# Linear attention's v and r products with 512 moving columns, r multiplied in behind the transposes, and the last turns' transposes at other steps

## The chip, the cores and the metric

The kernel is one program on one core of a Trainium2 chip. The metric is device time in microseconds (us), the median of the runs shown. The engines are called TensorE (PE; its weight loads are PEld), VectorE (DVE), ScalarE (ACT), GpSimd (POOL) and SyncE (SP, which issues nearly all DMAs here).

## The reference, cut to what matters

One layer of a decoder trunk over 1024 tokens of width 1024. A normalised input h is projected once; two mixers, gated DeltaNet (GDN) and gated linear attention (GLA), use its columns; both are projected, merged by gates, projected again and added; an MLP with a squared relu follows. What the change touches most is GLA, with 4 heads, key width 128 and value width 256:

```python
def gla_branch(q, k, v, r, gate_lr, gate_w2, gate_b, norm_w):
    ...
    gate_logit = (gate_lr @ gate_w2.astype(gate_lr.dtype)).astype(jnp.float32) + gate_b.astype(jnp.float32)
    log_a = jax.nn.log_sigmoid(gate_logit) / GLA_TAU
    log_a = split_heads(log_a, GLA_HEADS, GLA_DK)
    o = gla_chunked(qh, kh, vh, log_a).transpose(0, 2, 1, 3)
    rg = jax.nn.silu(r.reshape(bsz, s, GLA_HEADS, GLA_DV).astype(jnp.float32))
    o = rms_norm_f32(o, norm_w) * rg
    return o.reshape(bsz, s, GLA_V).astype(q.dtype)
```

q, k, v, r and gate_lr (16 columns) are column blocks of h @ w_in. gla_chunked works through chunks of 64 tokens with a state of 128x256 per head. The MLP is `u = square(relu(h @ w_mlp_up))`, `x + rms_norm(u @ w_mlp_down)`, with h the normalised result of the mixer.

## The kernel before

Every large float32 product is made as three products of a high and a low part in the type F32R: high with high, high with low, low with high (`mm3`, L256). The parts of a weight slab are made on the chip: SP loads 256 KB into a buffer of `wraw` (4 of them), ScalarE casts it to `wh` (L237, in `split`), VectorE subtracts to get `wl` (L166 through `tt`). Of wh and wl there are three buffers each (`wsp`). The activations' parts are `hT` and `hL`, with features on the partitions and tokens along the row.

Two forms of product exist. In `gemm_fm_` the weights are stationary and 512 tokens move: the result has features on the partitions, and each slab feeds 24 matmuls of 128x512. In `gemm_tm_` (L305) a block of 128 tokens is stationary and 256 weight columns move: the result has tokens on the partitions, and each slab feeds 48 matmuls of 128x256. Results go to four PSUM banks called g; the rest of the work has one bank each called mt, ml, mr and mo.

The GLA part (from L783) runs two streams at once. The main stream is the projections in the order of GORDER (k0 is head 0's q and k, v0 and r0 its v and r, g5 a block of merge-gate logits). The other is the attention proper, woven in between by `drive` (L76) with a virtual clock of TensorE (`TensorClock`): `ball_pair` for two heads' decays (a product of the low-rank gate input `sm` with `gw2`, in float32 on L68; then an exponential and a logarithm over 128x2048 on ScalarE, `e1s`, and a running sum on VectorE), `gla_mix` for one head, `gla_out` for its output. A table `need` says which of these must be over before a projection is started.

For each head and each half u of the tokens, gla_mix makes the attention matrix, and in two groups g of two token blocks the output in bank mo or ml. Each group is then squared and summed on ScalarE (into `jk`, a discard), its inverse root is taken on GpSimd (`so`, L172 and L186), and VectorE multiplies the group by it and by silu(r) into `gr` (L175, tokens on the partitions). When a head is done, gla_out transposes gr (TensorE, L72), ScalarE scales it by the norm's weight (`ot`), and SP writes it to DRAM (`d_ob`).

After the mixer comes the turn stage. The normalised mixer output `m` (tokens on the partitions) is transposed for the MLP. `turn(u, i)` does that for one of eight token blocks: two groups of four transposes to banks mt and ml, then copies and differences on ScalarE and VectorE into blocks `R` (`hilo`, L1096), `X` and two of `big`. The up-projection is arranged by Strassen's scheme over halves, which is what the differences are for. The turns of the second half stand between the steps of a loop of 16 (P1 and P2, 12 matmuls of 128x512 a step, banks mr and mo), and TURNS names the steps: TURNS[0] for u=0 in the projection before, TURNS[1] for u=1 in the loop. After the loop `prep(0)` loads the first up-weights into a buffer `wu` that X had until then (L1073), sums them on VectorE (`ss`), and the next products start from their casts.

Of the kernel before, what the change touches and what calls it, by code (L numbers as in the profile page):

```python
# [16 lines left out]
P = 128  # L17
S = 1024
# [8 lines left out]
TURNS = (2, 5, 6, 9), (3, 6, 10, 12)  # L27
# [4 lines left out]
GORDER = "k0 v0 r0 k1 v1 r1 k2 v2 r2 k3 v3 r3 g5"  # L32
# [101 lines left out]
def kernel(  # L134
# [30 lines left out]
    def tt(out, a, b, op, eng=None):  # L165
        (eng or V).tensor_tensor(out=out, in0=a, in1=b, op=op)  # L166
# [162 lines left out]
    sm = gp.tile([112, S], F32, name="sm")  # L329
# [51 lines left out]
    def decays(cv):  # L381


        ws = cv.tile([P, KT, 24], F32, name="ws", tag="Xc")
# [393 lines left out]


    with tc.tile_pool(name="gl", bufs=1, reuse_waits="tile") as gl:  # L780

        reserve(gl, (("gq", 512, 3), ("gk", 512, 3), ("gvh", S, 3), ("gvl", S, 3), ("gr", S, 4)))
        gw2 = gl.tile([112, 512], F32, name="gw2")  # L783
        V.memset(gw2, 0.0)
        for r in (32, 96):
            SP.dma_start(out=gw2[r:r + 16, :], in_=gla_gate_w2[0])
# [10 lines left out]
        def ball_pair(hh):  # L797

            lap = ball.rearrange("p h (u i) -> p (h u) i", u=2)
            for n in range(4):  # L800
# [4 lines left out]
                T.matmul(pl_, gw2[:, h * P:(h + 1) * P], sm[:, u * 512:u * 512 + 512], start=True, stop=True)  # L805
# [22 lines left out]
        def gla_v(h):  # L828
            bvv = yield from gemm_tm_(win_slab(C_BV + h * 256), KT, hT, hL)
            vs = [[gl.tile([P, 4, 256], F32R, tag="gv" + x, name="gv" + x, bufs=3) for x in "hl"] for _ in range(2)]  # L830
            for j in range(4):
                hi, lo = (v_[:, (j % 2) * 2:(j % 2) * 2 + 2, :].rearrange("p t c -> p (t c)") for v_ in vs[j // 2])
                with tc.high_priority(offset=HPE):
                    A.copy(out=hi, in_=bvv[j])
                    tt(lo, bvv[j], hi.bitcast(F32), ALU.subtract)
            vg[h] = vs

        def gla_r(h):
            brr = yield from gemm_tm_(win_slab(C_BR + h * 256), KT, hT, hL)
            rr = [gl.tile([P, 4, 256], F32, tag="gr", name="gr", bufs=4) for _ in range(2)]  # L840
            for j in range(4):
                rt3 = rr[j // 2][:, (j % 2) * 2:(j % 2) * 2 + 2, :]
                rt = rt3.rearrange("p t c -> p (t c)")
                with tc.high_priority(offset=HPE):
                    act(rt, brr[j], AF.Tanh, scale=0.5)
                    stt(rt, rt, 1.0, brr[j], ALU.add, ALU.mult)
            rg[h] = rr

        def gla_mix(h, mark):
            (qs, ks), vs = qkg[h], vg[h]  # L850
            st = None
            for u in range(2):
# [55 lines left out]
                vH, vL = vs[u]  # L908
                so = gl.tile([P, 4], F32, tag="so", name="so", bufs=2)
                jk = gl.tile([P, 2, 256], F32, tag="ot", name="jk", bufs=1)  # L910
                for g in range(2):
# [11 lines left out]
                    for j in range(2):  # L923
# [5 lines left out]
                        if j < nd:  # L929
# [608 lines left out]
```

## Time and profile before

| what | value |
|---|---|
| runs | 1704.4 us median of 3 (1701.24 to 1704.83) |
| the profiled execution | 1699.28 us, span 1697.5 us |
| granted TensorE clock, mean | 0.994 |
| PE / DVE / ACT / POOL busy | 97% / 58% / 45% / 8% of the span |

A matmul's own duration is longer than the distance between the starts of two in a row, since they are pipelined. In the list of waits the columns are: engine and line, what it waited for, total us, times, longest us. In the timeline they are start, duration, engine, line, operation, output and inputs with shapes, and in brackets the idle time before and what ended it. In the groups they are minimum, median and maximum in ns, and first and last start in us. In the table by stretches they are the length, the busy time of each engine, the granted TensorE clock (PEclk, 1.00 at full speed), the DMA engines' busy share and GB/s. The GLA part lies at about 434 to 822 us, the turn stage's loop at 1060 to 1112 us.

### The profile page before, as it was taken

Reading aid. Unit: us, or ns where it says so; the run is one execution under the profiler, and the core shown is the slowest. Engines: PE = TensorE matmul, PEld = TensorE weight load, DVE = VectorE, ACT = ScalarE, POOL = GpSimd, SP = SyncE. Lnnn points to the kernel's source line nnn. Section 1 sums busy time; section 2 is a strip of 40 time slices with the busy share of each in tenths; the row PEclk is TensorE's granted clock in tenths of the full one; section 3 lists DMA queues with packets and bytes.
Section 4 is the critical chain, followed back from the end, with each engine's and each line's share of the span. In section 5 each row is a group of like instructions: output and inputs, shape, how many; then the busy total and the mean of one; then the engine's idle time right before and its main releaser. Section 6 shows DMA issues by size and latency. Waiting matters only on the chain.

```text
span 1697.5 us, 24475 instructions
## 1 busy us (share of the span) xinstructions
PE 1653.0 (97%) x9174; PEld 1403.0 (83%) x9174; DVE 987.2 (58%) x1678; ACT 771.5 (45%) x1576; POOL 135.9 (8%) x222
## 2 busy tenths in 40 slices
PE   7999999999999999999999999989999999999997
PEld 6888778878898989998888888778888878888886
DVE  5677565872445335643354545798777655564764
ACT  5456554643533335433421235654555555443442
POOL 3010111111001000001100011200000000000021
PEclk9999999999999999999999999999999999999999
DMA  5222213322211212122743345687678698786763
GB/s 168 56 73 76 84 38 90 92 59 67 79 45 38 69 43 58 38 63 87 235 150 97 111 159 174 212 263 231 205 258 281 240 334 307 243 272 221 249 224 136
DMA packets 186405, 251.39 MB, mean 148 GB/s; under 512 B 23351, under 2 KB 108430, under 8 KB 186286
## 3 DMA queue, kind: packets, MB, share of 16 engines
q1 hardware_dynamic: 186286, 249.83, 45.7%
q8 instruction: 72, 1.18, 0.3%
q14 instruction: 47, 0.39, 0.1%
HBM read 185.79 MB, written 63.98 MB: 147 GB/s over the span
## 4 chain that ended last, share of the span: by engine, by line
PE 82%; DVE 7%; DMA 4%; ACT 4%; issue 2%; POOL 1%; SPq 0%; DVEq 0%; ACTq 0%; POOLq 0%
PE g L68 58%; PE mr L68 8%; PE mo L68 7%; PE ml L68 4%; PE mt L68 3%; DMA gb<-d_g 2%; DVE Xt L166 1%; PE mt L72 1%; DVE Xi L548 1%; DVE wl L166 1%; ACT E L178 1%; DMA oraw<-d_oa 1%; ACT wh L237 0%; DMA rv<-in_w_mlp_down_dram 0%; ACT Zp L604 0%
## 5 line engine op out<-in xcount | busy, mean ns | idle before, releaser
L166 DVE TENSOR_TENSOR wl<-w,wh 128x512 fp32r<-128x512 f32 x181 | 125.6, 695 | 223.5 <-ACT wh L237 220.0
L68 PE MATMUL g<-hT,wh 128*128 128x512 f32 (+1 forms) x600 | 239.1, 399 | 1.2 <-DVE gr L175 0.9
L68 PE MATMUL g<-hL,wh 128*128 128x512 f32 (+1 forms) x600 | 232.8, 388 | 0.0
L68 PE MATMUL g<-hT,wl 128*128 128x512 f32 (+1 forms) x600 | 232.1, 387 | 0.0
L237 ACT CAST wh<-w 128x512 fp32r<-128x512 f32 x184 | 113.8, 619 | 208.0 <-PE g L68 175.0
L68 PE MATMUL g<-wh,hT 128*128 128x256 f32 x640 | 185.7, 290 | 0.0
L68 PE MATMUL g<-wl,hT 128*128 128x256 f32 x640 | 182.1, 284 | 0.0
L68 PE MATMUL g<-wh,hL 128*128 128x256 f32 x640 | 182.0, 284 | 0.0
L68 PE MATMUL g<-big 128*128 128x512 f32 x768 | 175.3, 389 | 1.7 <-ACT big L1231 1.6
L68 PEld LDWEIGHTS g<-big 128*128 128x128 f32 x768 | 144.0, 188 | 32.3 <-ACT big L1231 2.0
L166 DVE TENSOR_TENSOR big<-ru,big 128x1024 fp32r<-128x1024 f32 x53 | 64.9, 1225 | 114.6 <-ACT big L1231 114.2
L68 PEld LDWEIGHTS g<-hT,wl 128*128 128x128 f32 x600 | 113.4, 189 | 21.6 <-DVE wl L166 0.2
L68 PEld LDWEIGHTS g<-hT,wh 128*128 128x128 f32 x600 | 113.4, 189 | 21.5 <-DVE gr L175 1.1
L68 PEld LDWEIGHTS g<-hL,wh 128*128 128x128 f32 x600 | 113.8, 190 | 18.8 <-issue 1.0
L1231 ACT CAST big<-ru 128x1024 fp32r<-128x1024 f32 x53 | 55.8, 1053 | 153.1 <-PE g L68 56.6
L68 PEld LDWEIGHTS g<-wh,hT 128*128 128x128 f32 x640 | 123.1, 192 | 1.4 <-issue 1.0
L68 PEld LDWEIGHTS g<-wl,hT 128*128 128x128 f32 x640 | 123.2, 193 | 1.2 <-issue 1.0
L68 PEld LDWEIGHTS g<-wh,hL 128*128 128x128 f32 x640 | 123.1, 192 | 0.1
L68 PE MATMUL g<-wh,big 128*128 128x512 f32 x256 | 81.1, 393 | 0.2 <-DVE m L166 0.2
L68 PE MATMUL g<-big,wh 128*128 128x512 f32 x256 | 78.8, 389 | 0.0
L178 ACT ACTIVATE c<-c 128x512 f32<-128x512 f32 x104 | 64.1, 630 | 21.8 <-DVE c L166 20.1
L166 DVE TENSOR_TENSOR big<-rv,big 128x1024 fp32r<-128x1024 f32 x53 | 64.6, 1218 | 0.2
(450 smaller groups left out, 3377.1 us busy)
## 6 DMA issues: line engine op xcount, KB each, us to landing
ru<-d_u SPq DMA_DIRECT2D x53, 512.0 KB, 4.6
w<-in_w_in_dram SPq DMA_DIRECT2D x80, 256.0 KB, 2.7
rv<-in_w_mlp_down_dram SPq DMA_DIRECT2D x37, 512.0 KB, 5.4
wu<-in_w_mlp_up_dram SPq DMA_DIRECT2D x32, 512.0 KB, 5.6
d_u<-c SPq DMA_DIRECT2D x56, 256.0 KB, 2.9
d_u<-us SPq DMA_DIRECT2D x48, 256.0 KB, 3.3
us<-in_w_mlp_down_dram SPq DMA_DIRECT2D x48, 256.0 KB, 4.4
xt<-in_x_dram SPq DMA_DIRECT2D x16, 512.0 KB, 5.4
```

Of the source, the lines that this page charges most:

```text
L68: return self.eng.matmul(out, lhsT, rhs, start=start, stop=stop, skip_group_check=more)
L72: return self.eng.transpose(out=out, in_=in_, identity=identity)
L166: (eng or V).tensor_tensor(out=out, in0=a, in1=b, op=op)
L178: A.activation(out=out, in_=a, func=func, **kw)
L237: A.copy(out=hi, in_=raw)
L548: V.tensor_reduce(out=X[:, :, i:i + 1], in_=tv, axis=AX.X, op=ALU.add)
L1231: A.copy(out=s4[:, i], in_=raw)
```

## The change

- v is computed for a pair of heads and half of the tokens at a time, in four calls of 96 matmuls in which 512 weight columns move; each slab of 256 KB (128 rows by 512 columns) feeds 12 matmuls. The parts gvh and gvl are then made in pieces of 128x256.
- r is computed by gemm_fm_, so that its result has features on the partitions.
- gla_mix squares into `on`, and scales by the inverse root into the same tile on ScalarE; one group later the four transposes of on follow, and VectorE multiplies their result by the norm's weight and silu(r) into gr, from which SP writes d_ob.
- The gate's product is made once in F32R: the high and low parts of gate input (`smr`) and gate weights stand on different rows of the same 112, 16 rows each, so that one product sums the three.
- TURNS and GORDER have new values, and the transposes of the second half of the turns use the four g banks.

```diff
-TURNS = (2, 5, 6, 9), (3, 6, 10, 12)
+TURNS = (2, 4, 6, 8), (2, 4, 6, 8)
...
-GORDER = "k0 v0 r0 k1 v1 r1 k2 v2 r2 k3 v3 r3 g5"
+GORDER = "k0 v0 r0 v1 k1 r1 k2 v2 r2 v3 k3 r3 g5"
...
-            for c, r, n in ((0, 0, 8), (8, 32, 16)):
+            for c, n, rh, rl in ((0, 8, (0,), 64), (8, 16, (16, 32, 80), 96)):
                 wv = ws[:, :, c:c + n]
-                A.copy(out=wx[:, :, r:r + n], in_=wv)
-                tt(wx[:, :, r + 64:r + 64 + n], wv, wx[:, :, r:r + n].bitcast(F32), ALU.subtract)
+                for r in rh:
+                    A.copy(out=wx[:, :, r:r + n], in_=wv)
+                tt(wx[:, :, rl:rl + n], wv, wx[:, :, rh[0]:rh[0] + n].bitcast(F32), ALU.subtract)
...
-            A.copy(out=sm[:, us], in_=ps[0:112, :])
+            A.copy(out=sm[0][:, us], in_=ps[0:72, :])
+            A.copy(out=smr[:, us], in_=ps[0:112, :])
+            tt(smr[64:96, us], ps[64:96, :], smr[64:96, us].bitcast(F32), ALU.subtract)
...
+    def load_slab512(ap, pool, tag, bufs=None):
+        raw = wraw.tile([P, 2, 256], F32, tag="w", name="w")
+        raw_ = raw.rearrange("p k c -> p (k c)")
+        SP.dma_start(out=raw_ if len(ap.shape) == 2 else raw, in_=ap)
+        raw = raw_
+        return split(raw, [P, 512], pool, tag, bufs)
...
+        gw = wraw.tile([P, 2, 256], F32, tag="w", name="w").rearrange("p a c -> p (a c)")[0:112]
+        gw2 = gl.tile([112, 512], F32R, name="gw2")
+        V.memset(gw, 0.0)
+        for r in (16, 32, 80, 96):
+            SP.dma_start(out=gw[r:r + 16, :], in_=gla_gate_w2[0])
+        A.copy(out=gw2, in_=gw)
+        tt(gw2[0:32], gw[0:32], gw2[0:32].bitcast(F32), ALU.subtract)
...
-                T.matmul(pl_, gw2[:, h * P:(h + 1) * P], sm[:, u * 512:u * 512 + 512], start=True, stop=True)
+                T.matmul(pl_, gw2[:, h * P:(h + 1) * P], smr[:, u * 512:u * 512 + 512], start=True, stop=True)
...
-        def gla_v(h):
-            bvv = yield from gemm_tm_(win_slab(C_BV + h * 256), KT, hT, hL)
-            vs = [[gl.tile([P, 4, 256], F32R, tag="gv" + x, name="gv" + x, bufs=3) for x in "hl"] for _ in range(2)]
-            for j in range(4):
-                hi, lo = (v_[:, (j % 2) * 2:(j % 2) * 2 + 2, :].rearrange("p t c -> p (t c)") for v_ in vs[j // 2])
-                with tc.high_priority(offset=HPE):
-                    A.copy(out=hi, in_=bvv[j])
-                    tt(lo, bvv[j], hi.bitcast(F32), ALU.subtract)
-            vg[h] = vs
+        def gla_v(n):
+            h0, u = n // 2 * 2, n % 2
+            banks = [gbank() for _ in range(4)]
+            for kts in [(kt,) for kt in range(KT - 2)] + [(KT - 2, KT - 1)]:
+                w = {kt: load_slab512(win[:, kt, C_BV + h0 * 256:C_BV + h0 * 256 + 512], wsp, "w") for kt in kts}
+                for i in range(4):
+                    tsl = slice((u * 4 + i) * P, (u * 4 + i) * P + P)
+                    for kt in kts:
+                        mm3(banks[i], hT[:, kt, tsl], hL[:, kt, tsl], *w[kt], kt == 0, kt == KT - 1)
+                    if i % 2 or kts[-1] == KT - 1:
+                        yield
+            for e in range(2):
+                vg[h0 + e, u] = [gl.tile([P, 4, 256], F32R, tag="gv" + x, name="gv" + x, bufs=3) for x in "hl"]
+            for i in range(4):
+                for e in range(2):
+                    hi, lo = (v_[:, i, :] for v_ in vg[h0 + e, u])
+                    src = banks[i][:, e * 256:e * 256 + 256]
+                    with tc.high_priority(offset=HPE):
+                        A.copy(out=hi, in_=src)
+                        tt(lo, src, hi.bitcast(F32), ALU.subtract)
         def gla_r(h):
-            brr = yield from gemm_tm_(win_slab(C_BR + h * 256), KT, hT, hL)
-            rr = [gl.tile([P, 4, 256], F32, tag="gr", name="gr", bufs=4) for _ in range(2)]
-            for j in range(4):
-                rt3 = rr[j // 2][:, (j % 2) * 2:(j % 2) * 2 + 2, :]
-                rt = rt3.rearrange("p t c -> p (t c)")
-                with tc.high_priority(offset=HPE):
-                    act(rt, brr[j], AF.Tanh, scale=0.5)
-                    stt(rt, rt, 1.0, brr[j], ALU.add, ALU.mult)
+            brr = yield from gemm_fm_(win_slab(C_BR + h * 256), KT, hT, hL)
+            rr = [[gl.tile([P, 512], F32, tag="gr", name="gr", bufs=8) for _ in range(2)] for _ in range(2)]
+            for e in range(2):
+                for u in range(2):
+                    rt = rr[e][u]
+                    with tc.high_priority(offset=HPE):
+                        act(rt, brr[e][u], AF.Tanh, scale=0.5)
+                        stt(rt, rt, 1.0, brr[e][u], ALU.add, ALU.mult)
             rg[h] = rr
+        left = []
+        def gla_out(mark):
+            h, u, g, on, t0 = left.pop()
+            yield max(0.0, t0 + GNORM - T.t)
+            while h not in rg:
+                yield LAT
+            pt = mbank("t").rearrange("p (e c) -> p e c", e=2)
+            for e in range(2):
+                for j in range(2):
+                    T.transpose(out=pt[:, e, j * P:j * P + P], in_=on[:, j, e * P:e * P + P], identity=ident)
+            cs = slice(g * 256, g * 256 + 256)
+            for e in range(2):
+                rt = rg[h][e][u]
+                stt(rt[:, cs], pt[:, e, :], chan[:, 53 + e:54 + e], rt[:, cs], ALU.mult, ALU.mult)
+                if g:
+                    SP.dma_start(out=d_ob[h * 2 + e, :, u * 512:u * 512 + 512], in_=rt)
+            if u and g:
+                mark("o%d" % h)
...
+                while (h, u) not in vg:
+                    yield LAT
+                vH, vL = vg[h, u]
...
+                    t0 = T.t
+                    if left:
+                        yield from gla_out(mark)
+                    on = gl.tile([P, 2, 256], F32, tag="on", name="on", bufs=1)
                     for j in range(2):
                         i = i0 + j
-                        act(jk[:, j, :], pb_[:, j, :], AF.Square, accum_out=so[:, i:i + 1])
+                        act(on[:, j, :], pb_[:, j, :], AF.Square, accum_out=so[:, i:i + 1])
                     sg_ = so[:, i0:i0 + 2]
                     rsqrt(sg_, sg_, 1.0 / 256, EPS)
-                    while h not in rg:
-                        yield LAT
-                    rr = rg[h]
                     for j in range(2):
                         i = i0 + j
-                        stt(rr[u][:, i, :], pb_[:, j, :], so[:, i:i + 1], rr[u][:, i, :], ALU.mult, ALU.mult)
+                        act(on[:, j, :], pb_[:, j, :], AF.Copy, scale=so[:, i:i + 1])
+                    left.append((h, u, g, on, t0))
                 mark("m%du%d" % (h, u))
-        def gla_out(h):
-            rr = rg[h]
-            for u in range(2):
-                us = slice(u * 512, u * 512 + 512)
-                for e in range(2):
-                    yield OUTW
-                    pt = mbank("t")
-                    for i in range(4):
-                        T.transpose(out=pt[:, i * P:(i + 1) * P], in_=rr[u][:, i, e * P:(e + 1) * P], identity=ident)
-                    ot = gl.tile([P, 512], F32, tag="ot", name="ot", bufs=1)
-                    act(ot, pt, AF.Copy, scale=chan[:, 53 + e:54 + e])
-                    SP.dma_start(out=d_ob[h * 2 + e, :, us], in_=ot)
...
-        need = {"k2": [("m0", 0)], "k3": [("m1", 0)], "v1": [("m0u0", 0)], "v2": [("m1u0", 0)], "v3": [("m2u0", 0)],
+        need = {"k2": [("m0", 0)], "k3": [("m1", 0)], "v1": [("m0u0", 0)], "v2": [("m1u0", 0), ("m0u1", 0)],
+                "v3": [("m1u1", 0), ("m2u0", 0)],
                 "r2": [("o0", 0)], "r3": [("o1", 0)]}
...
-            jobs.append(("o%d" % h, [("m%d" % h, GNORM)], lambda mark, h=h: gla_out(h)))
+        jobs.append(("end", [("m%d" % (H - 1), 0)], gla_out))
...
-                pt = mbank("tl"[g])
+                pt = gbank() if u else mbank("tl"[g])
```

The order of the instructions that results, at four places. The first is TensorE in GLA, where a head's normalised output is transposed. mt, ml and g are banks, gsh and gsl the parts of the state, qdh and qdl those of the decayed q. Before:

```order
L68 MATMUL g_5627<-wl_5686,hT_108 128x256
L68 MATMUL g_5627<-wh_5685,hL_109 128x256
L72 MATMUL mt_5719<-ident_77,gr_5311 128x128 x4
L68 MATMUL g_5627<-wh_5685,hT_108 128x256
L68 MATMUL g_5627<-wl_5686,hT_108 128x256
L68 MATMUL g_5627<-wh_5685,hL_109 128x256
```

After:

```order
L68 MATMUL g_5452<-hT_108,wl_5538 128x512
L68 MATMUL ml_5554<-gsh_5566,qdh_5241 128x256
L68 MATMUL ml_5554<-gsl_5567,qdh_5241 128x256
L68 MATMUL ml_5554<-gsh_5566,qdl_5242 128x256
L72 MATMUL mt_5582<-ident_77,on_5527 128x128 x4
L68 MATMUL g_5453<-hT_108,wh_5537 128x512
L68 MATMUL g_5453<-hL_109,wh_5537 128x512
```

Before, all four groups of a head stood in later projections, each with the finished gr; now a group of on stands directly behind the next group's last product.

The second is ScalarE at the same place: squares of a group, scaling, casts of slabs (wh) and of the state (gsh). Before:

```order
L178 ACTIVATE jk_5506,so_5505<-mo_5523 128x256 x2
L178 ACTIVATE e1s_4605<-d1_6292 128x512
L822 ACTIVATE gq_5621<-g_5322 128x512
L178 ACTIVATE e1s_4605<-ball_4604 128x512
L253 CAST gsh_5595<-gs_5593 128x256
L823 COPY gk_5618<-g_5323 128x512
L237 CAST wh_5747<-w_5745 128x512
```

After:

```order
L237 CAST wh_5636<-w_5633 128x512
L178 ACTIVATE on_5527,so_5467<-mo_5484 128x256 x2
L178 ACTIVATE on_5527<-mo_5484,so_5467 128x256 x2
L253 CAST gsh_5566<-gs_5564 128x256
L178 ACTIVATE on_5589,so_5467<-ml_5554 128x256 x2
L178 ACTIVATE on_5589<-ml_5554,so_5467 128x256
L237 CAST wh_5678<-w_5676 128x512
```

The scaling on<-mo,so, which reads GpSimd's so, now stands in ScalarE's queue between the squares and the next casts.

The third is VectorE in the turn stage, from the second half's first turn on. m is the normalised output, xt the residual, R22 and wu the blocks that the turn makes, ml or g the bank with the transposes. Before:

```order
L175 SCALAR_TENSOR_TENSOR m_10057<-xt_10477,rs_10481,wpre2_9671 128x1024
L175 SCALAR_TENSOR_TENSOR xt_10490<-m_10059,rs_10486,xt_10490 128x1024
L166 TENSOR_TENSOR wl_10698<-w_10695,wh_10697 128x512
L166 TENSOR_TENSOR wu_9668<-ml_10588,wu_9665 128x4x128
L166 TENSOR_TENSOR wu_9665<-wu_9665,wu_9666 128x4x128
L175 SCALAR_TENSOR_TENSOR m_10059<-xt_10490,rs_10494,wpre2_9671 128x1024
L166 TENSOR_TENSOR wl_10720<-w_10717,wh_10719 128x512
L166 TENSOR_TENSOR R22_9654<-ml_10588,R22_9654 128x4x128
L166 TENSOR_TENSOR wu_9666<-wu_9668,wu_9666 128x4x128
```

After:

```order
L175 SCALAR_TENSOR_TENSOR xt_9865<-m_9445,rs_9861,xt_9865 128x1024
L166 TENSOR_TENSOR wu_9056<-g_9954,wu_9053 128x4x128
L166 TENSOR_TENSOR wu_9053<-wu_9053,wu_9054 128x4x128
L175 SCALAR_TENSOR_TENSOR m_9445<-xt_9865,rs_9869,wpre2_9059 128x1024
L166 TENSOR_TENSOR wl_10064<-w_10061,wh_10063 128x512
L175 SCALAR_TENSOR_TENSOR xt_9878<-m_9447,rs_9874,xt_9878 128x1024
L166 TENSOR_TENSOR wl_10107<-w_10104,wh_10106 128x512
L166 TENSOR_TENSOR R22_9042<-g_9954,R22_9042 128x4x128
L166 TENSOR_TENSOR wu_9054<-wu_9056,wu_9054 128x4x128
```

The turn's subtractions read a g bank rather than ml, and still stand among the m<-xt rows of later blocks.

The fourth is SP at the end of the loop: d_u and d_p are the loop's results in DRAM, w its weight slabs, wu the first up-weights behind it. Before:

```order
L1174 DMA w_10913<-in_w_mlp_up_dram 128x4x128
L1192 DMA d_p_102<-e_10758 128x512
L1192 DMA d_u0_93<-e_10800 128x512
L1192 DMA d_u0_93<-e_10822 128x512
L1192 DMA d_p_102<-e_10866 128x512
L1192 DMA d_p_102<-e_10888 128x512
L1073 DMA wu_10935<-in_w_mlp_up_dram 128x8x128 x2
```

After:

```order
L1210 DMA w_10279<-in_w_mlp_up_dram 128x4x128
L1228 DMA d_p_102<-e_10166 128x512
L1210 DMA w_10301<-in_w_mlp_up_dram 128x4x128
L1228 DMA d_p_102<-e_10188 128x512
L1109 DMA wu_10323<-in_w_mlp_up_dram 128x8x128
L1228 DMA d_u0_93<-e_10209 128x512
L1109 DMA wu_10323<-in_w_mlp_up_dram 128x8x128
```

The first load of wu came behind the writes of the results; now it comes right behind the last slab's load and one write.

More of the change, by code (lines that the diff above doesn't have):

```diff
@@ L327 @@
     gp = tc.alloc_tile_pool(name="gp", bufs=1, reuse_waits="tile")
-    sm = gp.tile([112, S], F32, name="sm")
+    sm = {}
+    smr = gp.tile([112, S], F32R, name="smr")
     bt = gp.tile([P, NTOK, 8], F32, name="bt")
@@ L381, in decays @@
     def decays(cv):
+        sm[0] = cv.tile([72, S], F32, tag="C", name="sm", bufs=2)
         ws = cv.tile([P, KT, 24], F32, name="ws", tag="Xc")
@@ L407, in decays2 @@
             for t in range(4):
-                T.transpose(out=pb[:, t, :], in_=sm[0:72, (g * 4 + t) * P:(g * 4 + t + 1) * P], identity=ident[0:72, 0:72])
+                T.transpose(out=pb[:, t, :], in_=sm[0][:, (g * 4 + t) * P:(g * 4 + t + 1) * P], identity=ident[0:72, 0:72])
             V.tensor_copy(out=bt[:, g * 4:g * 4 + 4, :], in_=pb[:, :, 0:8])
@@ L777 @@
         drive(T, main[1:], lanes, ["q0"])
-    with tc.tile_pool(name="gl", bufs=1, reuse_waits="tile") as gl:
[L782 to L786, printed above, removed]
+    def load_slab512(ap, pool, tag, bufs=None):
[4 more added lines that the diff above has]
+        return split(raw, [P, 512], pool, tag, bufs)
+    with tc.tile_pool(name="gl", bufs=1, reuse_waits="tile") as gl:
+        reserve(gl, (("gq", 512, 3), ("gk", 512, 3), ("gvh", S, 3), ("gvl", S, 3), ("gr", 512, 8)))
+        gw = wraw.tile([P, 2, 256], F32, tag="w", name="w").rearrange("p a c -> p (a c)")[0:112]
[5 more added lines that the diff above has]
+        tt(gw2[0:32], gw[0:32], gw2[0:32].bitcast(F32), ALU.subtract)
         smask = gl.tile([P, 8, 64], F32, name="smask")
@@ L849, in gla_mix @@
         def gla_mix(h, mark):
-            (qs, ks), vs = qkg[h], vg[h]
+            qs, ks = qkg[h]
             st = None
@@ L907, in gla_mix @@
                 atH, atL = split_ps(at, gl, "at", 1)
-                vH, vL = vs[u]
+                while (h, u) not in vg:
+                    yield LAT
+                vH, vL = vg[h, u]
                 so = gl.tile([P, 4], F32, tag="so", name="so", bufs=2)
-                jk = gl.tile([P, 2, 256], F32, tag="ot", name="jk", bufs=1)
                 for g in range(2):
@@ L972 @@
                 jobs.append(("b%d" % h, [], lambda mark, h=h: ball_pair(h)))
-            jobs.append(("m%d" % h, [("v%d" % h, 2.0), ("k%d" % h, 2.0), ("b%d" % (h // 2 * 2), BW if h % 2 == 0 else 0)],
+            jobs.append(("m%d" % h, [("v%d" % (h // 2 * 2), 2.0), ("k%d" % h, 2.0), ("b%d" % (h // 2 * 2), BW if h % 2 == 0 else 0)],
                          lambda mark, h=h: gla_mix(h, mark)))
-            jobs.append(("o%d" % h, [("m%d" % h, GNORM)], lambda mark, h=h: gla_out(h)))
+        jobs.append(("end", [("m%d" % (H - 1), 0)], gla_out))
         drive(T, main, {"t": jobs})
@@ L1037 @@
                     tt(mg_[u][1][:, c * 2 + b, :], mg, mg_[u][0][:, c * 2 + b, :].bitcast(F32), ALU.subtract)
-    def load_slab512(ap, pool, tag, bufs=None):
-        raw = wraw.tile([P, 2, 256], F32, tag="w", name="w")
-        raw_ = raw.rearrange("p k c -> p (k c)")
-        SP.dma_start(out=raw_ if len(ap.shape) == 2 else raw, in_=ap)
-        raw = raw_
-        return split(raw, [P, 512], pool, tag, bufs)
     sgp.release()
```

## The prediction

> **What bounds the kernel now.** I read the page's sums and its chain first, then the list of waits, then the timeline of TensorE where the change touches it, and last the table by stretches.
>
> ```profile
> span 1697.5 us, 24475 instructions
> PE 1653.0 (97%) x9174; PEld 1403.0 (83%) x9174; DVE 987.2 (58%) x1678; ACT 771.5 (45%) x1576; POOL 135.9 (8%) x222
> PE 82%; DVE 7%; DMA 4%; ACT 4%; issue 2%; POOL 1%; SPq 0%; DVEq 0%; ACTq 0%; POOLq 0%
> ```
>
> TensorE is busy for 97% of the span and carries 82% of the chain: a saving counts if it shortens TensorE's own row of work or ends one of its few waits. Work added to VectorE or ScalarE counts only where TensorE then waits for it. The waits that the change can reach:
>
> ```profile
> PE ml L72 <- DVE R L166: 2.4, 1, 2.4
> PE mr L68 <- ACT wh L237: 4.7, 1, 4.7
> PE g L68 <- DVE gr L175: 0.9, 1, 0.9
> DVE gr L175 <- POOL so L186: 24.8, 14, 2.7
> ```
>
> The first two lie in the MLP's turn stage, the third in linear attention. The fourth costs nothing today: VectorE waits there, off the path.
>
> ```profile
> core 0: us, PE busy (x) PEld busy (x) DVE busy (x) ACT busy (x) POOL busy (x), PEclk, DMA share, GB/s
> 434.00:850.00 416.00, 414.79 (x2851) 376.52 (x2850) 187.46 (x336) 167.08 (x330) 35.87 (x56) 1.00 0.26 75
> 970.00:1059.00 89.00, 88.77 (x404) 72.44 (x404) 46.57 (x66) 40.66 (x82) 11.34 (x20) 1.00 0.50 164
> ```
>
> Linear attention (the first stretch) keeps TensorE busy for 414.79 of 416 us with VectorE at 45% and ScalarE at 40%, so its instruction count is its time. The second stretch already uses one 256 KB weight slab for twelve matmuls of 512 columns, and TensorE loses 0.23 us in 89 there.
>
> **Term 1, 512 moving columns for v and r.** Four v calls and four r calls issue 192 matmuls of 128x256 each, 1536 in all; after, 768 of 128x512. The price is the spacing of starts (the durations overlap):
>
> ```profile
> 656.96 0.28 PE L68 MATMUL g<-wh,hT 128*128 128x256 f32 x1
> ...
> 662.96 0.28 PE L68 MATMUL g<-wh,hL 128*128 128x256 f32 x1
> ```
>
> ```profile
> 436.13 0.39 PE L68 MATMUL g<-hT,wl 128*128 128x512 f32 x1
> ...
> 439.53 0.39 PE L68 MATMUL g<-hT,wl 128*128 128x512 f32 x1
> 439.76 1.02 PE L68 MATMUL mt<-sm,gw 112*128 112x512 f32 x2
> 440.21 0.80 PE L68 MATMUL g<-hT,wh 128*128 128x512 f32 x1
> 440.85 0.40 PE L68 MATMUL g<-hL,wh 128*128 128x512 f32 x1
> ```
>
> Between the first pair lie 50 steps: 6.00/50 = 0.1200 us. Between the next pair 15: 3.40/15 = 0.2267. Two small ones cost 0.2400 against 0.2267 for a large one, and 768 times 0.0133 is **10.2 us**, all on the path. [...]
>
> What it adds lies beside TensorE: v's slabs go from 16 to 32, so 16 more casts and subtractions; the group counts for both today:
>
> ```profile
> L237 ACT CAST wh<-w x57: 599/620/632, 438.5 to 817.6; 128x512 fp32r<-128x512 f32 x57
> L166 DVE TENSOR_TENSOR wl<-w,wh x58: 667/692/1787, 433.6 to 818.4; 128x512 fp32r<-128x512 f32 x58
> ```
>
> That is 16 x 0.62 = 9.9 us of ScalarE and 16 x 0.69 = 11.1 us of VectorE, plus 16 loads of 256 KB on SP's queue, in engines idle for more than half the stretch: nothing on the path while the cover holds. The cover: three slab buffers exist, so the next slab is being split while two are used, 2 x 2.72 us (12 x 0.2267 each) less 0.62 and 0.69, or 4.1 us. A v slab lasted 48 x 0.12 = 5.76 us before. If ScalarE or VectorE is held for more than 4.1 us, TensorE waits.
>
> **Term 2, the gate product.** Today's f32 product of 512 columns issues two records. From 439.76 to 440.85 pass 1.09 us for it and one ordinary matmul; less 0.23 it costs 0.86. As one F32R pass it costs 0.23. Eight of them: 8 x 0.63 = **5.0 us**. Its extra splitting (two ScalarE casts of 512 columns, two small subtractions, the copies of wx) lies in the GDN stage, where the added work on each engine is below 3 us and its consumer comes much later; I cost it at nothing, and at 1 us for the range.
>
> **Term 3, r behind the transposes.** TensorE transposes 16 groups of four before and after. What changes is who waits:
>
> ```profile
> L178 ACT ACTIVATE jk<-mo x16: 368/378/388, 506.4 to 786.2; 128x256 f32<-128x256 f32 x16
> L172 POOL TENSOR_SCALAR so<-so x16: 192/193/425, 507.3 to 793.0; 128x2 f32<-128x2 f32 x16
> L186 POOL TENSOR_TENSOR so<-so,mhalf x16: 697/698/707, 507.6 to 793.3; 128x2 f32<-128x2 f32 x16
> L175 DVE SCALAR_TENSOR_TENSOR gr<-mo,so,gr x16: 473/478/485, 511.9 to 788.2; 128x256 f32<-128x256 f32 x16
> L178 ACT ACTIVATE ot<-mt,chan x16: 685/688/692, 553.3 to 804.0; 128x512 f32<-128x512 f32 x16
> ```
>
> ScalarE gains 32 scaling copies (priced like the squares, 0.38: 12.1 us) and loses 16 evictions of 0.69 (11.0 us). VectorE keeps 32 multiplications of 128x256. The 0.9 us wait for gr goes, since those rows no longer hold a buffer that the r product needs: **0.9 us**. But the copy waits in ScalarE's queue for POOL's square root, on average 24.8/14 = 1.8 us at today's VectorE, and slab casts and state casts (gsh) stand behind it. 1.8 is under the cover of 4.1. The single buffer of normalised output is read a whole group later, so it holds nothing back except at the end, where about 18 matmuls (4.1 us) stand between the last product and its transposes, against two squares, POOL and two copies of about 3.7: 0 to 0.7 us.
>
> The place where the cover is thinnest is the second pair's decay, now beside v2's slabs. Its work on ScalarE today:
>
> ```profile
> 657.23 1.91 ACT L178 ACTIVATE e1s<-e1s 128x2048 f32<-128x2048 f32 x1
> 659.05 0.60 ACT L237 CAST wh<-w 128x512 fp32r<-128x512 f32 x1
> 659.67 1.28 ACT L178 ACT_TABLE_LOAD   x1
> 660.96 1.92 ACT L178 ACTIVATE e1s<-e1s 128x2048 f32<-128x2048 f32 x1
> ```
>
> In the changed order no cast stands between the first and the last of these: 1.91 + 1.28 + 1.92 = 5.1 us, one above the cover. For linear attention I take new waits of **2.0 us** (bounds 0 and 6: three stalls of two).
>
> **Term 4, the turn stage.** Transposes of the second half go to four banks rather than to one pair, and to steps 2, 4, 6, 8 rather than 3, 6, 10, 12.
>
> ```profile
> 1060.67 0.62 PE L68 MATMUL mr<-R,wh 128*128 128x512 f32 x2
> ...
> 1080.61 0.60 PE L72 MATMUL mt<-ident,m 128*128 128x128 f32 x4
> 1083.63 0.63 PE L72 MATMUL ml<-ident,m 128*128 128x128 f32 x4 [2.42 <-DVE R L166]
> ...
> 1111.79 0.39 PE L68 MATMUL mo<-R,wl 128*128 128x512 f32 x1
> 1116.85 1.22 PE L68 MATMUL mr<-big,wh 128*128 128x512 f32 x2 [4.67 <-ACT wh L237]
> ```
>
> ```profile
> 1083.60:1087.75 4.15, 4.12 (x13) 3.33 (x14) 4.12 (x7) 2.16 (x4) 0.00 (x0) 0.59 0.75 230
> 1116.85:1122.17 5.32, 5.32 (x12) 3.80 (x13) 5.32 (x10) 2.04 (x4) 0.00 (x0) 0.53 1.10 367
> 1122.17:1125.00 2.83, 2.83 (x14) 2.35 (x13) 1.90 (x4) 0.70 (x2) 0.00 (x0) 1.00 1.13 349
> ```
>
> Each idle time was followed by a stretch at a granted clock of 0.59 or 0.53. Twelve matmuls took 5.32 us where twelve take 2.72: 2.6 lost. After the first idle, nine matmuls took 3.74 (1084.01 to 1087.75) for 2.04: 1.7 lost. Both places together cost 2.42 + 1.7 + 4.67 + 2.6 = 11.4 us.
>
> ```profile
> 1080.99 1.29 DVE L175 SCALAR_TENSOR_TENSOR m<-xt,rs,wpre 128x1024 f32<-128x1024 f32 x1 [0.71 <-POOL rs L186]
> 1109.02 1.01 SPq L1073 DMA_DIRECT2D wu<-in_w_mlp_up_dram  x2
> 1116.18 1.14 ACT L237 CAST wh<-ss 128x512 fp32r<-128x512 f32 x2 [2.33 <-DVE ss L166]
> ```
>
> The first wait exists because the subtraction that frees bank l stands on VectorE behind this m<-xt row; with four banks the second block's transposes need no freeing, and the wait goes. The second exists because the first up-weights are loaded into a buffer that the last turn still reads: issued at 1109.02, first matmul 7.83 us later. With the last turn at step 8 the issue moves to about 1099 to 1101 (behind the loop's last slab load on SP's queue), so the weights are usable at 1107 to 1109. The loop starts at 1060.67; 16 steps of 2.72 and four turns of 0.8 end at 1107.4. VectorE becomes nearly as tight as TensorE there, since four turns' subtractions now fall in 16 us rather than 24. I leave 2.0 us (bounds 0 and 7.4) of the 11.4: **9.4 us**.
>
> **Sum.** 10.2 + 5.0 + 0.9 - 2.0 + 9.4 = 23.5 us. The profiled execution took 1699.28 us (span 1697.5), 5.1 below the median 1704.4 of the three runs; from it the sum gives 1675.8, from the median 1680.9. I forecast **1681 us** as the median.
>
> **Rivals.**
> (a) The 13 ns that a pair loses belong to the moving columns, not to the instruction, and a large matmul of v or r, whose stationary block changes each time, comes at nearly twice 0.1200. [...] For it speaks that no v or r row of 512 columns exists yet; against it, that the q and k rows of 512 columns above also change their stationary block each time and hold 0.2267 over fifteen steps. [...]
> (b) VectorE is the bound in the turn stage: the idle moves to the loop's end with its slow clock. If 4.8 us of idle and slow clock stay beyond the 2.0 (a stall of 4.67 with 2.1 more), term 4 is 4.6: 1686. For it: VectorE was busy 53.3 of 66 us there by the stretch below; against: its work does not grow.
>
> ```profile
> 1059.00:1125.00 66.00, 58.91 (x258) 47.81 (x257) 53.30 (x74) 43.39 (x81) 11.80 (x20) 0.92 0.69 225
> ```
>
> (c) Slower: v's slabs come late. ScalarE's copy, held by POOL, holds the casts behind it, and each of v's 32 slabs must now arrive every 2.72 us. A stall like 1083.63 costs 2.42 and 1.7 of clock, 4.1. Without the allowance the gain is 25.5, so from 25.5/4.1 = 6.2 such stalls the change loses; eight, one slab in four, give 1704.4 - 25.5 + 32.8 = 1712. Against it: 970 to 1059 runs at this rate without a loss, and 1.8 is under 4.1.
> (d) Half of it: the same late slabs at three or four places, 12 to 16 us: 1691 to 1695.
>
> **Chances.** The forecast's case (1674 to 1686) 0.58; (a) 0.06; (b) 0.18; (d) 0.11, of which 0.03 end within 0.2% of 1704.4; (c) 0.07, with 0.01 of that within. A measurement here tells a change from none at about 0.2%, 3.4 us. Faster 0.90, same 0.04, slower 0.06. The low end takes the profiled execution's scale with no new wait at all: 1699.3 - 10.2 - 5.0 - 0.9 - 11.4 = 1671.8; the high end takes (d) with 2 us more, 1697.
>
> **What would show it.** Right: 128x512 rows of v and r 0.227 apart; smr,gw rows single; no idle before the turn stage's second transposes, and the first matmul of the up-weights by 1109 minus what the earlier stages saved; PEclk 1.0 between. Wrong: TensorE waits for wl or wh inside v1, v2 or v3; a row of 128x512 that is spaced more than 0.235; a slow clock at the loop's end. A gain under 14 us would mean that terms 1 or 4 failed.

## The result, and the profile after

The changed kernel takes 1681.93 us (median of 4, 1680.9 to 1682.86) against 1704.39 us (median of 4, 1701.24 to 1704.83): ratio 0.9872, interval 0.9855 to 0.9889, 22.5 us faster. Its profiled execution took 1681.06 us with a span of 1679.3, so the two profiled executions differ by only 18.2 us. Most of the rest lies in how far before's profiled execution stood below its median (1699.28 under 1704.39); this matters below.

The page of the changed kernel, the same rows as before:

```profile
span 1679.3 us, 23070 instructions
PE 1636.7 (97%) x8398; PEld 1356.9 (81%) x8398; DVE 1001.2 (60%) x1713; ACT 785.6 (47%) x1629; POOL 134.9 (8%) x222
PE 78%; DVE 8%; DMA 5%; ACT 5%; issue 2%; POOL 1%; SPq 1%; DVEq 0%; ACTq 0%; POOLq 0%
```

VectorE and ScalarE each gained 14 us of work, and TensorE has 776 rows fewer and is still busy for 97%. Linear attention, from its first gate product to the first product of the projection behind it, before and after:

```profile
439.76:837.97 398.21, 397.00 (x2772) 361.81 (x2770) 182.75 (x330) 159.42 (x317) 31.42 (x49) 1.00 0.24 70
```

```profile
439.01:825.01 386.00, 383.27 (x1995) 318.99 (x1994) 199.06 (x365) 175.12 (x370) 31.16 (x50) 1.00 0.29 85
```

It is 12.2 us shorter, at an unchanged clock. TensorE's idle time in it went from 1.2 to 2.7 us. The list of waits in this stretch:

```profile
PE g L68 <- ACT sg L178: 1.1, 1, 1.1
PE g L68 <- DVE gvl L166: 0.8, 2, 0.5
PE g L68 <- ACT gk L841: 0.4, 1, 0.4
PE ml L68 <- ACT on L178: 0.4, 1, 0.4
```

None of these is a wait for a slab (wh or wl). The gvl rows are v's evictions, which hold the next call's banks; on is the new scaling, which holds bank ml once for 0.37 us; sg is the sigmoid of the merge gates at the end of the stretch, for which before waited 0.29 us.

In the turn stage the loop of 16 steps now starts at 1047.27. Two of its four turns and the first up-weights, from TensorE's timeline, and three stretches of it:

```profile
1055.43 1.03 PE L72 MATMUL g<-ident,m 128*128 128x128 f32 x8
1074.50 1.03 PE L72 MATMUL g<-ident,m 128*128 128x128 f32 x8
1075.96 0.73 PE L68 MATMUL mo<-R,wh 128*128 128x512 f32 x2 [0.42 <-ACT e L178]
...
1085.36 0.72 PE L68 MATMUL mr<-R,wh 128*128 128x512 f32 x2 [0.68 <-ACT e L178]
...
1097.45 0.73 PE L68 MATMUL mr<-big,wh 128*128 128x512 f32 x2 [0.64 <-ACT e L178]
```

```profile
1074.50:1080.00 5.50, 5.08 (x26) 3.86 (x25) 5.46 (x10) 4.76 (x10) 0.00 (x0) 1.00 0.64 204
1080.00:1085.40 5.40, 4.72 (x22) 3.57 (x20) 5.40 (x10) 4.62 (x9) 0.00 (x0) 1.00 0.38 126
1085.40:1091.00 5.60, 5.60 (x24) 4.32 (x25) 5.60 (x8) 5.60 (x10) 0.00 (x0) 1.00 0.78 232
```

All eight transposes of a turn now run as one row. The waits of 2.42 and 4.67 us and the slow clock are gone; in their place stand three waits under 0.7 us for a relu (e) that comes late, while VectorE is busy for 16.46 of 16.5 us. From the loop's start to the first g<-big row of the down projection pass 307.5 us (1047.27 to 1354.79) where 314.6 passed before (1060.67 to 1375.29): 7.1 us gained. Then something is given back. The down projection's first wait, in the changed kernel:

```profile
1379.33 20.84 PE L68 MATMUL g<-big 128*128 128x512 f32 x82 [2.38 <-ACT big L1267]
```

```profile
1380.00:1385.00 5.00, 4.94 (x15) 3.62 (x14) 4.83 (x5) 4.09 (x5) 0.00 (x0) 0.66 1.03 409
```

Before, the same place had an idle time of 1.62 us at full clock:

```profile
1398.96 27.85 PE L68 MATMUL g<-big 128*128 128x512 f32 x120 [1.62 <-ACT big L1231]
1400.00:1405.00 5.00, 4.94 (x22) 3.97 (x22) 4.83 (x5) 4.12 (x5) 0.00 (x0) 1.00 1.04 415
```

From the first g<-big row to the first mt<-big row passed 51.4 us before and 53.8 after: 2.5 us lost, in a stage that no line of the diff touches.

### The profile page after: what moved, and what is told of

Its sections match the earlier page's. It is cut to its first block, busy times and chain, and to the rows that moved or that the text cites. A ratio compares the mean times of both kernels' runs of the same rounds, so it can differ in the third digit from the quotient of the medians.

```text
span 1679.3 us, 23070 instructions
## 1 busy us (share of the span) xinstructions
PE 1636.7 (97%) x8398; PEld 1356.9 (81%) x8398; DVE 1001.2 (60%) x1713; ACT 785.6 (47%) x1629; POOL 134.9 (8%) x222
## 4 chain that ended last, share of the span: by engine, by line
PE 78%; DVE 8%; DMA 5%; ACT 5%; issue 2%; POOL 1%; SPq 1%; DVEq 0%; ACTq 0%; POOLq 0%
PE g L68 57%; PE mr L68 7%; PE mo L68 6%; PE ml L68 4%; PE mt L68 3%; DVE Xt L166 1%; DMA gb<-d_g 1%; PE mt L72 1%; DVE wl L166 1%; DVE Xi L555 1%; DMA oraw<-d_oa 1%; ACT wh L237 1%; DMA w<-in_w_in_dram 1%; ACT Zp L611 0%; DMA us<-in_w_mlp_down_dram 0%
## 5 line engine op out<-in xcount | busy, mean ns | idle before, releaser
L68 PE MATMUL g<-hT,wh 128*128 128x512 f32 (+1 forms) x728 | 288.8, 397 | 2.0 <-ACT sg L178 1.1
L68 PE MATMUL g<-hL,wh 128*128 128x512 f32 (+1 forms) x728 | 282.4, 388 | 0.0
L68 PE MATMUL g<-hT,wl 128*128 128x512 f32 (+1 forms) x728 | 282.1, 388 | 0.0
L68 PEld LDWEIGHTS g<-hT,wh 128*128 128x128 f32 x728 | 137.5, 189 | 26.6 <-ACT sg L178 1.5
L68 PE MATMUL g<-wh,hT 128*128 128x256 f32 (+1 forms) x256 | 87.1, 341 | 0.4 <-ACT gk L841 0.4
L68 PE MATMUL g<-wl,hT 128*128 128x256 f32 (+1 forms) x256 | 86.7, 339 | 0.0
L68 PE MATMUL g<-wh,hL 128*128 128x256 f32 (+1 forms) x256 | 86.5, 338 | 0.0
L68 PE MATMUL g<-R,wh 128*128 128x512 f32 x192 | 59.3, 390 | 0.0
L68 PEld LDWEIGHTS g<-big,wh 128*128 128x128 f32 x256 | 48.0, 188 | 11.3 <-DVE c L166 1.4
L68 PEld LDWEIGHTS g<-wh,big 128*128 128x128 f32 x256 | 48.0, 188 | 11.2 <-DVE m L166 1.1
```

Of the source, the lines that this page charges most:

```text
L68: return self.eng.matmul(out, lhsT, rhs, start=start, stop=stop, skip_group_check=more)
```

## Experiments

The runs were made in three groups, each with before on the same chip. Before took 1700.6, 1700.0 and 1700.9 us there (medians of 29, 11 and 18 runs, single runs from 1695.3 to 1704.0), where the four runs of the result had a median of 1704.4. Ratios are to before on the same chip. In what follows "linear attention" is the stretch shown above, measured in each trace.

### The parts alone

The turns alone: TURNS and the one line in turn().

```diff
-TURNS = (2, 5, 6, 9), (3, 6, 10, 12)
+TURNS = (2, 4, 6, 8), (2, 4, 6, 8)
-                pt = mbank("tl"[g])
+                pt = gbank() if u else mbank("tl"[g])
```

> Before, with the new steps of the turns and their four banks alone. Theory (the gain by stage adds up): the loop of the turn stage loses its 2.42 and 4.67 us waits and their slow clock and keeps small waits, as the changed kernel's trace shows: 7.1 us gained up to the first row of the down projection, so about 1697 if that stage's first wait stays at 1.6 us at full clock. Rival (the gain is given back): the first wait of the down projection grows to 2.4 us with a slow clock behind it, as in the changed kernel's trace, and only 4.6 us remain: about 1700.

Measured: 1695.38 us, ratio 0.9968 (0.9957 to 0.9979), 5.2 us. From the loop to the down projection the trace is 6.4 us shorter (308.2 against 314.6), and the down projection's first wait is the longest that any of these traces shows:

```profile
PE g L68 <- ACT big L1231: 3.8, 1, 3.8
```

Both halves of what was expected are there: the gain of the stage, and a part of it given back one stage later. The new steps and the new banks were not run apart.

The gate's product alone: the hunks of decays, gw2 and ball_pair.

```diff
-                T.matmul(pl_, gw2[:, h * P:(h + 1) * P], sm[:, u * 512:u * 512 + 512], start=True, stop=True)
+                T.matmul(pl_, gw2[:, h * P:(h + 1) * P], smr[:, u * 512:u * 512 + 512], start=True, stop=True)
```

> Before, with the gate's product in one F32R pass alone. Theory: eight products fall from 0.86 to 0.23 us, 5.0 us in all, and nothing else moves: about 1699. Rival: the extra splits of the gate input in the GDN stage delay TensorE there by 1 us or more and 4 us or less remain: 1700 or more.

Measured: 1698.44 us, ratio 0.9991 (0.9982 to 1.0000): 2.1 us between the medians, near the limit of what can be told. In the trace the g rows and the gate rows of linear attention together lose 5.1 us (from 347.9 to 342.9, starts counted and idle time left out), as expected; the wait for sg at its end is 1.4 us longer, the wait for R in the turn stage 3.7 instead of 2.4 us, and the down projection's first wait 3.6. The GDN stage is not later (its first gate product starts at 438.35 against 439.76), so the rival's reason did not occur. In this trace the gain was there and was spent on waits elsewhere.

v alone: gla_v and its order of calls; r and the mix as before. The entries of the table `need` for v2 and v3 also stay as before, here and where v and r are run together, though the expectation speaks of the changed kernel's needs.

```diff
-GORDER = "k0 v0 r0 k1 v1 r1 k2 v2 r2 k3 v3 r3 g5"
+GORDER = "k0 v0 r0 v1 k1 r1 k2 v2 r2 v3 k3 r3 g5"
-        def gla_v(h):
+        def gla_v(n):
...
```

> Before, with v alone in 512 columns (its order of calls and its needs as in the changed kernel), r as before. Theory: half of what the two traces show for v and r, 7.9/2 = 4.0 us, less waits of about 1.3 us for slabs and bank evictions: 2 to 4 us gained, 1700 to 1702. Rival (c) of the prediction in small: slabs at 2.72 us come late, some waits of over 2 us for wl or wh, no gain or a loss.

Measured: 1703.2 us, ratio 1.0018 (1.0007 to 1.0029): slower by 2.6 us. Linear attention is 4.2 us longer. Its waits, and the stretch behind the first of them:

```profile
PE g L68 <- ACT sg L178: 2.1, 1, 2.1
PE ml L68 <- DVE gr L175: 1.5, 1, 1.5
PE ml L68 <- DVE ki L166: 1.5, 1, 1.5
PE g L68 <- ACT gk L830: 0.6, 1, 0.6
```

```profile
820.20:824.50 4.30, 4.27 (x12) 3.41 (x13) 1.46 (x3) 1.78 (x3) 1.32 (x2) 0.61 0.75 244
```

Neither theory gave this. No row waits for wl or wh, so the slabs at 2.72 us are not late. Bank ml waits for the multiplication with r that still reads it (gr), and once the attention's product of qi and ki waits for ki, which stands on VectorE among the rows that finish r: 3.0 us for the two. The largest part is the wait for sg, 1.8 us longer than before, with 1.65 us of slow clock behind it. That part is not surely v's: the wait for sg was 0.3 us in before's trace and 1.1 with the turns alone, whose linear attention is the same. Without sg and its slow clock v alone would be longer than before by an estimated 0.8 us rather than 4.2.

r alone: gla_r by gemm_fm_, and multiplied in behind the transposes.

```diff
-            brr = yield from gemm_tm_(win_slab(C_BR + h * 256), KT, hT, hL)
+            brr = yield from gemm_fm_(win_slab(C_BR + h * 256), KT, hT, hL)
...
+                        act(on[:, j, :], pb_[:, j, :], AF.Copy, scale=so[:, i:i + 1])
```

> Before, with r alone by the form with stationary weights, and multiplied in behind the transposes; v as before. Theory: 4.0 us from the larger matmuls and 0.9 us from the wait for gr that goes: about 1699 to 1700. Rival: the scaling in ScalarE's queue, which waits for GpSimd, delays the casts behind it, and TensorE waits for wl, gsl or on: under 3 us gained.

Measured: 1695.14 us, ratio 0.9969 (0.9958 to 0.9980), 5.4 us; linear attention 4.7 us shorter, with 1.05 us of waits in all. The wait for gr is gone and no wait for on or a slab has come.

The four ratios alone add up to 9 us of gain, half of what the whole change brings.

### v and r together, the turns undone, and the change again

v and r together, the old gate and the old turns (the hunks of the two experiments above):

```diff
+        def gla_v(n):
+            brr = yield from gemm_fm_(win_slab(C_BR + h * 256), KT, hT, hL)
...
```

> Before, with v and r together as in the changed kernel; the old gate product and the old turns. The experiment with v alone lost 4.2 us in linear attention by its trace, the one with r alone gained 4.7. Theory: v alone loses only because its calls stand ahead of r's and the attention multiplies r in at once, so that a bank and a slab buffer wait (gr, ki); with r behind the transposes these waits go, and linear attention gains about 8 us. Ratio 0.994 to 0.996. Rival: v's late slabs cost the same beside the new r, the two add up to about 0.5 us, ratio 0.999 to 1.001.

Measured: 1692.59 us, ratio 0.9957 (0.9945 to 0.9968), 7.4 us. Linear attention:

```profile
439.11:829.44 390.33, 387.88 (x2004) 320.56 (x2002) 200.17 (x367) 175.86 (x371) 32.03 (x50) 1.00 0.28 84
```

7.9 us less than before, where v alone is 4.2 more and r alone 4.7 less. The waits for gr and ki are gone. So in the traces v takes off 3.2 us more with r behind the transposes, and nothing without it. The run times are less clear on these 3.2 us, since the intervals of r alone and of v and r overlap. That the held bank makes the difference is read from the waits that are gone; no run shows it by itself.

The changed kernel with the old turns, and the changed kernel again:

```diff
-TURNS = (2, 4, 6, 8), (2, 4, 6, 8)
+TURNS = (2, 5, 6, 9), (3, 6, 10, 12)
-                pt = gbank() if u else mbank("tl"[g])
+                pt = mbank("tl"[g])
```

> The changed kernel with the old steps of the turns and the old banks. Theory: 5 to 6 us of the gain lie in the turn stage, as with the turns alone (ratio 0.9968), so the ratio to before is about 0.990 where the whole change has 0.987. Rival: in the changed kernel the turn stage starts at another time and without the idle time the old steps cost less: 0.988 or less.

> The changed kernel again, on the chip of these comparisons. Theory: 0.987 as measured first, 22 us, of which the parts alone (turns 0.0032, gate 0.0009, v -0.0018, r 0.0031) explain only 9 us; the rest then belongs to v and r together. Rival: the first ratio holds for its chip only and here it comes out near the parts' sum, 0.993 to 0.995.

Measured: 1687.38 us, ratio 0.9927 (0.9916 to 0.9939), without the turns; 1681.58 us, ratio 0.9893 (0.9880 to 0.9905), for the change again. Taken one after the other on one chip, v and r bring 7.4 us, the gate 5.2 (1692.59 to 1687.38), the turns 5.8 (1687.38 to 1681.58), and these steps make up the whole 18.4 by construction. What can be compared is each step with the same edit alone: v and r 7.4 us where the two alone come to 2.8, the gate 5.2 where it brought 2.1, the turns 5.8 where they brought 5.2. The step of the gate also has the new entries of `need`; in the traces its 4.6 us in linear attention all lie in the g and gate rows (339.3 to 334.7), so those entries show no effect there. The changed kernel takes the same time as at first (1681.93); before doesn't (1704.4 and 1700.0). Its single runs spread over 9 us, those of the changed kernel over 2, so a median of four is less sure for before. The first chip may also run before more slowly, which was not tested. 18 to 19 us, from the later runs, is the better supported gain.

### The wait that gave some back

```diff
-        SP.dma_start(out=wpost2, in_=norm_mlp_post[0].unsqueeze(0).broadcast_to([P, D]))
...
         plain("P1", Ab, True)
...
+        SP.dma_start(out=wpost2, in_=norm_mlp_post[0].unsqueeze(0).broadcast_to([P, D]))
         ts(wpost2, wpost2, D ** 0.5, ALU.mult, eng=G)
```

> The changed kernel with the load of the last norm's weights (a broadcast of 128x1024 on SP, ahead of the first ru loads of the down projection) moved behind the first product's loads. Its trace waits 2.38 us there for ru and then runs at a granted clock of 0.66. Theory: ru lands about 1 us earlier, the wait falls under 1.7 us and the slow stretch (1.7 us) goes with it: 2.5 to 3 us faster than the changed kernel, ratio 0.985 or 0.986. Rival: the DMA engines are the limit whatever the order, 1 us or nothing.

Measured: 1677.88 us (1677.62 to 1679.75), ratio 0.9873 (0.9860 to 0.9886), 3.7 us below the changed kernel on the same chip, whose runs do not overlap with these (1680.92 to 1682.51). On ScalarE's and SP's timelines, from the first load's issue to the first cast that waits for it, in the changed kernel and here:

```profile
1369.53 0.45 SPq L1457 DMA_DIRECT2D wpost<-in_norm_mlp_post_dram  x1
1370.03 0.45 SPq L1250 DMA_DIRECT2D ru<-d_u  x1
1376.96 1.04 ACT L1267 CAST big<-ru 128x1024 fp32r<-128x1024 f32 x1 [12.51 <-DMA ru<-d_u]
```

```profile
1370.34 0.45 SPq L1250 DMA_DIRECT2D ru<-d_u  x1
1375.13 1.05 ACT L1267 CAST big<-ru 128x1024 fp32r<-128x1024 f32 x1 [9.55 <-DMA ru<-d_u]
```

6.9 us became 4.8, and the stretch that was slow has neither idle time nor a slow clock:

```profile
1375.00:1380.00 5.00, 5.00 (x23) 4.00 (x22) 3.55 (x3) 4.09 (x4) 0.00 (x0) 1.00 1.02 389
```

This version beats both kernels. The same move on the kernel before, and before again for a second trace of it:

> The kernel before again, with a new trace. Every experiment's trace so far has a longer first wait of the down projection (2.1 to 3.8 us, slow clock behind it) than the one trace of before (1.62, full clock). Theory: that trace was a lucky execution, a new one shows 2.4 us or more and 2 to 3 us more between the first g<-R and the down projection's first mt row; time ratio 1.000. Rival: before keeps its 1.6 us, and all edits, small as they are, lengthen that wait.

> The kernel before with only the load of the last norm's weights moved behind the first product's loads. Theory: the wait at the start of the down projection goes here too, with its slow clock, 4 us or more as in the changed kernel (0.9977). Rival: 1.6 us only, as the one trace of before shows (0.999).

Measured: before again 1699.2 us, ratio 0.9995 (0.9985 to 1.0004); with the late load 1696.23 us, ratio 0.9972 (0.9961 to 0.9982). The second trace of before has 1.84 us at that wait, at full clock:

```profile
1396.61 0.73 PE L68 MATMUL g<-big 128*128 128x512 f32 x2 [1.84 <-ACT big L1231]
```

This does not bear out the theory of a lucky first trace, but does not rule it out: both traced executions of before were fast ones (1699.28 under a median of 1704.4, and 1696.9, the lowest of its ten runs), and the late load gains 3.0 to 4.6 us by the runs (from 1699.2 or 1700.9) where the traces show 2.2 from the first g<-big row to the first mt<-big row (51.5 to 49.4). In both traces of before the wait is short, and in the eight traces of edited kernels that keep the early load it is 2.1 to 3.8 us. Why it is longer there is open; that the load's place removes it, with or without the change, is shown.

### Two tries at the turn stage

```diff
-                tt(x21, x21, x11, ALU.subtract)
+                tt(x21, x21, x11, ALU.subtract, eng=G)
```

> The changed kernel with the late load and, in each turn of the second half, one of VectorE's subtractions (x21 less x11) on GpSimd. The trace shows VectorE busy without a gap from 1067 to 1091 us in the turn stage and TensorE waiting there for e and c, 3.4 us lost in the loop. Theory (VectorE is the bound there): 4 x 0.6 us less on it, 1 to 2 us gained on the run with the late load alone, ratio 0.986. Rival: GpSimd's subtraction is slower than 2 us and what reads x21 next waits, or the loads of wu are what is late: no gain or a loss.

```diff
-TURNS = (2, 4, 6, 8), (2, 4, 6, 8)
+TURNS = (2, 4, 6, 8), (2, 5, 8, 10)
```

> The changed kernel with the late load and the second half's turns at steps 2, 5, 8 and 10. Theory (VectorE and ScalarE are crowded by four turns in seven steps): the waits for e in the loop, 2.6 us, fall, but the last turn frees the buffer of wu two steps (5.4 us) later and the first up-weights are late: a wait of 2 to 3 us before the first mr<-big row with a slow clock, 1 to 3 us slower than with the late load alone. Rival: the loads have 5 us to spare, and it is 1 to 2 us faster.

Measured: 1679.52 us, ratio 0.9872 (0.9859 to 0.9886), and 1678.97 us, ratio 0.9868 (0.9855 to 0.9882): neither can be told from the late load alone (0.9873). GpSimd's four subtractions took 1.29 to 2.22 us, and VectorE's rows beside three of them took longer, about 1.8 instead of 0.68 us twice and 2.30 instead of 1.28 once, so what was moved away came back. With the turns apart the first up-weights are late, as expected:

```profile
1098.58 0.73 PE L68 MATMUL mr<-big,wh 128*128 128x512 f32 x2 [2.14 <-ACT wh L237]
```

What the loop gains in shorter waits for e this wait takes back.

## Why the prediction was right, and where its steps were off

The forecast was 1681 us and the runs gave 1681.93. The steps, one by one, from the two profiled executions where no other run is named:

- **Term 1, 10.2 us for v and r.** The g rows of linear attention take 344.2 us before and 335.6 in the trace of v and r together (starts counted, idle time left out), 8.6 us or 11.3 ns for a pair instead of 13.3. The rows that gave the price came from undisturbed stretches; between other work the saving is smaller. The kind of the saving was right, and rival (a), a large matmul at nearly twice 0.1200, is out: v's rows of 512 columns follow each other at the same distance as those of q and k, 6.12 us for 27 steps or 0.2267.

```profile
469.81 0.39 PE L68 MATMUL g<-wl,hT 128*128 128x512 f32 x1
...
475.93 0.39 PE L68 MATMUL g<-wl,hT 128*128 128x512 f32 x1
```

- **Term 2, 5.0 us for the gate.** 4.6 us beside v and r, 5.1 alone. Rows that were 0.86 us with what follows are single:

```profile
439.01 0.40 PE L68 MATMUL mt<-smr,gw 112*128 112x512 f32 x1
439.24 0.40 PE L68 MATMUL g<-hT,wh 128*128 128x512 f32 x1
```

- **Term 3, 0.9 gained and 2.0 lost.** TensorE's idle time grew by 1.5 us, 0.4 more than the net of the two; 0.8 of it is the longer wait for sg, which the turns alone show too, so only the rest can be put down to the change with any certainty. The place was wrong: the second pair's decay holds ScalarE from 623.81 to 628.85, 5.0 us as estimated, and TensorE does not wait there. The cover of 4.1 us was too small an estimate: when the decay began one slab of v2 had just been started (623.09) and two more stood ready or nearly so, and the one behind them was needed at 631.25 only. Two sizes off the path were wrong as well. The copy's wait for so was 1.1 us on average, not 1.8, and from a group's first square to its last copy passed 2.8 us, not 3.7; TensorE never sat idle before a transpose of on.

```profile
623.28 0.62 ACT L237 CAST wh<-w 128x512 fp32r<-128x512 f32 x1
623.81 1.91 ACT L178 ACTIVATE e1s<-e1s 128x2048 f32<-128x2048 f32 x1
625.74 1.28 ACT L178 ACT_TABLE_LOAD   x1
627.03 1.92 ACT L178 ACTIVATE e1s<-e1s 128x2048 f32<-128x2048 f32 x1
628.85 1.12 ACT L237 CAST wh<-w 128x512 fp32r<-128x512 f32 x2
```

- **Term 4, 9.4 us of 11.4 for the turn stage.** 7.1 in the profiled pair, 5.2 and 5.8 by the runs, and only 3.3 between the second traces of the two kernels (312.8 us from the loop to the down projection in before, 309.5 changed). Both waits went as argued, and the first up-weights' matmul, at 1097.45, waits for bank mr (e) and not for its weights. In the profiled pair 4.3 us were left over rather than 2.0, 2.7 of them idle time in four small waits rather than one at the end. The 11.4 also held 1.7 of slow clock that the second trace of before does not have. Rival (b) said that VectorE would be the bound. It is busy for 16.96 of 17 us from 1074 to 1091, and TensorE waits there for e; but with the turns apart it is as busy in the same stretch, and TensorE does not wait at all (the line below). So a full VectorE is not enough to hold TensorE. The late relus stand on ScalarE between casts of the turns, some of which wait for VectorE; which order would end these waits is open.

```profile
1074.00:1091.00 17.00, 17.00 (x83) 13.97 (x83) 16.93 (x27) 15.45 (x29) 0.00 (x0) 1.00 0.42 143
```

- **Not in the sum.** 2.5 us are given back around the down projection's first wait. No step of the prediction looked at it, though 1.62 us stood in before's trace.
- **Rivals (c) and (d), slabs late.** No trace waits for a slab of v. What v alone waited for was another thing (gr, ki and sg), and the waits for gr and ki are gone with r changed.

By the terms as measured, 8.6 + 4.6 + 7.1, less 1.5 and 2.5, with 0.5 from the mix rows and 1.4 before and between the stages, the profiled pair differs by 18.2 us and not 23.5. That the number came out within 1 us has two causes. Most terms were of the right size. The other is luck: the sum, 5 us too large, was taken from a median of three runs, 1704.4, that stands 4 us above before's median in the later comparisons. From 1700.0 the same sum would have given 1676.5, 5 us too low.

## What to carry to other kernels

Count how far apart the starts of matmuls are over a whole stage rather than in its best stretch, and price every wait that stands in the trace behind the change, not only those the change touches: time saved ahead may be given back there. Two edits can be worth less apart than together; run them in pairs before dropping one. A load that is not needed until a whole product later can hold up the first loads of a stage by 2 us if it is issued just ahead of them (6.9 us against 4.8 here). What an idle time of about 2.5 us costs in clock can change from one execution to the next (0.59 behind 2.42 us in one trace of before, full clock behind 2.57 us at the same place in the other), so it should not be priced from a single trace.

## What was not expected of the hardware

The slow clock behind an idle time is not a matter of the length of that idle time alone. At the same place, before the second transposes of the same turn, the first trace of before was idle for 2.42 us and ran at 0.59 afterwards; the second trace of before was idle for 2.57 us and ran at full clock:

```profile
1083.11 0.63 PE L72 MATMUL ml<-ident,m 128*128 128x128 f32 x4 [2.57 <-DVE R L166]
1083.10:1087.20 4.10, 4.09 (x20) 3.48 (x21) 4.07 (x7) 3.05 (x6) 0.00 (x0) 1.00 0.73 224
```

From the loop's start to the down projection the second execution is 1.85 us shorter, about the 1.7 us that nine matmuls lost in the first. The longer idle time before the first up-weights was followed by a slow clock in both: 4.67 us by 0.53 in the first, 4.5 us by 0.50 in the second:

```profile
1114.50:1118.00 3.50, 3.46 (x8) 2.34 (x9) 3.50 (x7) 2.07 (x4) 0.00 (x0) 0.50 1.11 346
```

The down projection's first wait had full clock behind it in both traces of before (1.62 and 1.84 us), and 0.66 behind 2.38 us in the changed kernel's. So at 2.4 to 2.6 us both cases occur, and what decides between them is open.
